# A two-layer diffusion backbone on one core: where layer 0's second shift is computed, FFN tile 1, fills, and the last squares

## The chip, the cores and the metric

The kernel runs on one core of one Trainium2 chip. The metric is the device time of one execution in microseconds (us). Three timed runs of the kernel before took 3376.17, 3380.72 and 3391.68 us; the median is 3380.72.

The engines are named as in the profile: PE is TensorE (matmul), DVE is VectorE, ACT is ScalarE, POOL is GpSimd, and SP is SyncE, which here only issues DMAs, from one queue in order.

## What is computed

The kernel computes two layers on a stream of 1024 latent tokens and 256 context tokens with 1024 columns, and returns the latents after a last RMSNorm. Cut to what matters here, a layer of the reference is:

```python
mod = c_act @ w_ada[li] + b_ada[li]
sh1, sc1, g1, sh2, sc2, g2 = jnp.split(mod[:, None, :], 6, axis=-1)
# (the same with cc_act for the context tokens)
m = unpack(modulate(rms_norm(x, norm1_w[li]), sh1, sc1) @ w_in[li], lb_all[li])
att  = diff_head_norm(diff_attend_blocks(rope(q), k_all, v_all, lam), ...)   # 4 heads
rec  = hgrn_out(hgrn_bidir(...), ...)             # gated linear recurrence, 4 heads
four = fourier_mix(m['uf'], w_fnet[li])           # FNet: 2-D Fourier mixing
x = x + g1 * (concat(att, rec, four) @ w_out[li])
x = x + g2 * conv_ffn(modulate(rms_norm(x, norm2_w[li]), sh2, sc2),
                      w_up[li], conv_w[li], conv_b[li], w_down[li])
# after the last layer: rms_norm(x, final_norm_w)
```

`w_ada` is 1024 x 6144 in each layer. The six parts of `mod` are shift, scale and gate of the first norm, then shift, scale and gate of the second. In tiles of 128 outputs, 24 to 31 are the second shift, 32 to 39 the second scale, 40 to 47 the second gate.

## The kernel before

**Products.** All large products run as three products of parts: a weight is split into a rounded part `wh` and the rest `wl`, an activation into `hh` and `hl` (`mt`: both in one tile), and PE adds wh x hh, wh x hl and wl x hh. Weights come as 128 x 1024 tiles (`wr`); ACT makes `wh`, and POOL or DVE subtracts to get `wl`.

**Stages of a layer.** The norm; the input projection as `head(h)` (q and k of one attention head, tile `g`, L378), `gemm_v(j)` (values, tile `gv`, L395) and others, spilled to memory; between them the hgrn pairs 0 and 1 (`hgrn_pair`), whose small chains on DVE and ACT are covered by filling PE with projections (`fill0`, `fill1`); FNet (`vp` L822, `sp`, `pq`, `fps`); the rope work of each head, `late(h)`, which loads spilled q and k, rotates them on POOL and writes them to memory places `zk`, `zq`, `zl`; attention (scores `sp` L913, maximum on DVE, exponential on ACT, transposes `tp`, outputs `op` L961); the output projection (`wout_all`), with the second norm's squares beside it; the FFN's up phase (`phase_up`), 22 pairs of column tiles; the down phase (`phase_down`) in pairs of tiles.

**Memory.** Tiles come from pools that are opened and closed like a stack on two sides. The hgrn pool closes when the last instruction on its tiles is done. FNet's pool, the rope pool and the attention tiles take the place that it leaves.

**The adaLN product** is no matmul for most tiles: a row of the transposed weight block is multiplied on DVE with the broadcast condition and summed up in the same instruction. It is spread over the program as generators that are advanced from the code of other stages. `ada_halves` (layer 0, tiles 16 to 31, from the hgrn stage): a step is one load `adaq` of two tiles' quarter, 256 KB, and four products of 128 x 256 (L246: two tiles, two conditions); 32 steps, two load buffers, which it shares with hgrn's `kts`. `ada_wout` (layer 0, tiles 32 to 39, from the output projection): a load `adaw` of 512 KB and two products of 128 x 1024 a tile (L149). `ada_rest` (tiles 40 to 47 of layer 0 and 0 to 31 of layer 1, from layer 0's FFN): 160 steps of one load of 128 KB and one or two products of 128 x 256 (L223), advanced by `fill` behind certain DVE instructions of the up phase and by one behind each of the eight columns of a down pair.

**The up phase** uses a scheme with seven products in place of eight for a 2 x 2 block of weights: `begin` and `more` make the products pE and pA of a tile, `regular` makes pD, `second` the products on sums of weights (`q`) with sums of activations (`xt`, `t`, made by `Blocks` after the norm), pB and pE. `split` makes the two parts of a weight; every third of its results goes to an own tile `wl2`, which for layer 0 lies in the FFN pool. `context` (tile `gc`) is the plain product for the context tokens. `Rstd` gathers a norm's squares: ACT squares a column tile, DVE or POOL adds it to `acc` (L291) or it is left as a further part, and `finish` sums over the partitions with a matmul by ones (`ss`, L300) and makes the reciprocal root on ACT (L301, L302).

**Order.** The kernel is written with a tile framework whose scheduler simulates a timeline and from it sets the order of every engine's instructions; an engine then runs its list in order, and waits on semaphores where a tile isn't ready.

Of the kernel before, what the change touches and what calls it, by code (L numbers as in the profile page):

```python
# [75 lines left out]
def backbone(ctx: ExitStack, tc: tile.TileContext, xt, cvec, wada, wada0, win, winv, wout, wup, wdown, wfn,  # L76
# [200 lines left out]
    class Rstd:  # L277


        def __init__(self, acc, tmp):  # L280
            self.acc, self.tmp, self.seen, self.more = acc, tmp, set(), {}

        def add(self, x, t0, n, eng=None):
            r = slice(t0, t0 + n)
            if t0 in self.seen:
                sq = self.tmp(n)
                S.activation(out=sq[:, :n], in_=x[:, r], func=AF.Square)
                if eng is PE:
                    self.more.setdefault(t0, []).append(sq)
                    return  # L290
# [4 lines left out]

        def finish(self, ps, t0, n):
            r = self.acc[:, t0:t0 + n]
            parts = [r] + self.more.get(t0, [])
            for i, a in enumerate(parts):
                PE.matmul(ps[:, :n], lhsT=ones, rhs=a[:, :n], start=(i == 0), stop=(i == len(parts) - 1))  # L300
# [66 lines left out]
    def mixers(l, hs, hpool, epool, ep, hside, oside):  # L367
# [4 lines left out]
        with tc.tile_pool(name=f"psx{l}", bufs=3, space=PSUM) as psx, tc.tile_pool(name=f"psg{l}", bufs=3, space=PSUM) as psg:  # L372
# [32 lines left out]
            if True:  # L405
                with tc.tile_pool(name=f"hgrn{l}", bufs=1, side=oside) as gp:
                    mark("hgrn0")
                    ada = ada_halves(gp, 0, (0, 1), range(16, 32)) if l == 0 else none(gp)

                    def pace(*counts):  # L410
                        todo = iter(counts)

                        def also():
                            for _ in range(next(todo, 0)):
                                next(ada, None)
                        return also
                    hgrn_pair(l, 0, gp, psx, gemm, gemm_v, both, qch, pace(2, 2, 2, 1, 1))
                    mark("fill0")
                    also = pace(*[1] * 8)
# [4 lines left out]
                    hgrn_pair(l, 1, gp, psx, gemm, gemm_v, both, qch, list)  # L424
                    mark("fill1")
                    also = pace(*[2] * 5 + [1] * 6)
# [173 lines left out]
    def hgrn_pair(l, p, gp, psx, gemm, gemm_v, both, qch, also):  # L600
# [42 lines left out]
        if p == 0:  # L643
            gemm_v(2, also)
# [450 lines left out]
    def phase_up(l, blocks, psp, pcp, nrm, q, p1):  # L1095
# [19 lines left out]
        def split(x, r=slice(0, 1024)):  # L1115
            turn_w[0] += 1
            h = wp.tile([P, 1024], F32R, tag="wh", name="wh")
            w = (nrm if last else fp).tile([P, 1024], F32R, tag="wl2", bufs=1, name="wl") if turn_w[0] % 3 == 0 else wp.tile([P, 1024], F32R, tag="wl", bufs=2, name="wl")
# [37 lines left out]
        def more(j):  # L1156
            j.A = bank("pA")
            product(j.A, j.w1, 512, blocks.B21, True)
            j.c1 = context(j.w1)
            j.w1 = None  # L1160
# [58 lines left out]
        def gate(j):  # L1219
            j.g, done = conv(j.f, u1, j.c1)  # L1220
            fill(done, 1)
# [19 lines left out]
        more(j)  # L1241
        yield
        regular(j)
        ahead = None
        if last:
            ahead = begin(1)
            more(ahead)
# [8 lines left out]
        for f in range(1, NF):  # L1256
# [4 lines left out]
            if not ahead:  # L1261
                more(j)
            ahead = None
# [16 lines left out]
    def phase_down(l, xs, hs, psp, pcp, cvs, norm_of, acts, rest):  # L1280
# [11 lines left out]
        def down(fs):  # L1292
            ws = [(load_w(wdown[l, f]), a) for f, a in fs]
            for d in range(KD):
# [8 lines left out]
                fill(done, 1)  # L1303
# [413 lines left out]
```

## Time and profile before

| what | value |
|---|---|
| timed runs | 3376.17, 3380.72, 3391.68 us |
| profiled execution | 3365.03 us, its span 3363.2 us |
| mean granted TensorE clock | 0.962 |
| PE busy | 3073.5 us (91%) |
| DVE busy | 2407.3 us (72%) |
| ACT, POOL busy | 1389.9 us (41%), 1087.7 us (32%) |
| DMA | 397.75 MB, mean 118 GB/s |

How to read the views below. A *window* row gives its bounds and length in us, then the busy time (and the number of instructions) of PE, PEld (weight loads beside PE), DVE, ACT and POOL, the mean granted TensorE clock as a share of full speed (2.4 GHz), the DMA engines' busy share, and GB/s. The *clock slices* of the page cut the span into 40 parts of 84 us and give the clock in tenths. A *source* row gives line, engine, operation and tiles of a group, how often it ran, the shortest, median and longest duration in ns, the first and last start in us, and the shapes; under it stand the releasers of the idle time just before these instructions, in us and how often. A *wait* row says who waited for whom: us in total, how often, the longest. A *timeline* row gives start, duration, engine, line, operation and tiles, and in brackets the engine's idle time before it with what ended it. Large matmuls appear as two records for each instruction at full width.

The stages of layer 0 on the time axis of this execution: hgrn pair 0 with its fills to about 290, pair 1 to 470, FNet and the rest of the projections to 597, attention to 843, the output projection to 980, the FFN's up phase to about 1575, the down phase behind it.

### The profile page before, as it was taken

Reading aid. Unit: us, or ns where it says so; the run is one execution under the profiler, and the core shown is the slowest. Engines: PE = TensorE matmul, PEld = TensorE weight load, DVE = VectorE, ACT = ScalarE, POOL = GpSimd, SP = SyncE. Lnnn points to the kernel's source line nnn. Section 1 sums busy time; section 2 is a strip of 40 time slices with the busy share of each in tenths; the row PEclk is TensorE's granted clock in tenths of the full one; section 3 lists DMA queues with packets and bytes.
Section 4 is the critical chain, followed back from the end, with each engine's and each line's share of the span. In section 5 each row is a group of like instructions: output and inputs, shape, how many; then the busy total and the mean of one; then the engine's idle time right before and its main releaser. Section 6 shows DMA issues by size and latency. Waiting matters only on the chain.

```text
span 3363.2 us, 49615 instructions
## 1 busy us (share of the span) xinstructions
PE 3073.5 (91%) x19008; PEld 2562.8 (76%) x19008; DVE 2407.3 (72%) x3917; ACT 1389.9 (41%) x2360; POOL 1087.7 (32%) x742
## 2 busy tenths in 40 slices
PE   5899896799979999999899998998899899999998
PEld 3777775588867887877788786777787778887786
DVE  7467755698578888778877847763896877777546
ACT  5343421477244443334111453622673454444213
POOL 5253443561121111113432234444641111112643
PEclk8899997899989999999999998999999999999999
DMA  5223136665512222225432222136656222224421
GB/s 211 90 73 97 49 106 190 196 167 173 202 58 90 88 93 83 93 88 185 144 126 82 85 79 68 59 105 217 174 168 247 85 82 79 84 76 150 145 76 69
DMA packets 197505, 397.75 MB, mean 118 GB/s; under 512 B 21394, under 2 KB 94866, under 8 KB 197268
## 3 DMA queue, kind: packets, MB, share of 16 engines
q1 hardware_dynamic: 197268, 394.59, 36.1%
q8 instruction: 149, 2.44, 0.3%
q14 instruction: 88, 0.72, 0.1%
HBM read 284.66 MB, written 85.20 MB: 110 GB/s over the span
## 4 chain that ended last, share of the span: by engine, by line
PE 39%; DVE 17%; DMA 5%; issue 4%; ACT 2%; POOL 2%; SPq 0%; DVEq 0%; POOLq 0%; ACTq 0%
PE gl L1300 12%; PE pE L1129 7%; PE pB L1129 4%; DVE wl L1120 4%; PE g L378 3%; DMA wr<-wup 3%; PE gl L547 2%; PE gv L395 2%; DVE adaj L223 2%; PE pA L1129 2%; PE gc L1300 1%; DVE cv L1215 1%; PE op L961 1%; PE sp L913 1%; PE gl L1319 1%
## 5 line engine op out<-in xcount | busy, mean ns | idle before, releaser
L131 POOL TENSOR_TENSOR wl<-wr,wh 128x1024 fp32r<-128x1024 f32 x116 | 297.3, 2572 | 814.3 <-PE gc L1300 153.2
L1300 PE MATMUL gl<-mt,wh 128*128 128x512 f32 x1280 | 347.9, 396 | 15.2 <-DVE xs L1301 13.3
L1301 DVE SCALAR_TENSOR_TENSOR xs<-gl,mod,xs 128x512 f32<-128x512 f32 x336 | 235.8, 744 | 138.6 <-PE gl L1300 137.1
L129 ACT CAST wh<-wr 128x1024 fp32r<-128x1024 f32 x116 | 121.4, 1047 | 481.5 <-PE gc L1300 161.7
L1300 PEld LDWEIGHTS gl<-mt,wh 128*128 128x128 f32 x1280 | 235.7, 189 | 66.9 <-DVE xs L1301 16.8
L378 PE MATMUL g<-hh,wh 128*128 128x512 f32 (+1 forms) x696 | 257.3, 379 | 12.3 <-DVE w L597 9.2
L378 PE MATMUL g<-hl,wh 128*128 128x512 f32 (+1 forms) x696 | 255.8, 377 | 0.0
L1129 PE MATMUL pE<-mt,wh 128*128 128x512 f32 x704 | 229.8, 397 | 1.5 <-ACT u L1179 1.5
L915 DVE TENSOR_REDUCE mx<-sp 128x1 f32<-128x1280 f32 (+1 forms) x136 | 194.3, 1436 | 47.9 <-PE sp L913 47.2
L1120 DVE TENSOR_TENSOR wl<-wr,wh 128x1024 fp32r<-128x1024 f32 (+1 forms) x134 | 214.2, 1606 | 13.1 <-ACT wh L1119 7.5
L923 ACT ACTIVATE e<-sp,mx 128x1280 f32<-128x1280 f32 (+1 forms) x144 | 177.9, 1238 | 64.5 <-DVE mx L915 63.4
L1300 PE MATMUL gl<-mt,wl 128*128 128x512 f32 x640 | 190.8, 395 | 0.0
L1119 ACT CAST wh<-q 128x1024 fp32r<-128x1024 f32 x44 | 46.2, 1051 | 311.7 <-DVE q L1165 247.1
L961 PE MATMUL op<-vt,at 128*128 128x128 f32 x1312 | 161.3, 278 | 4.9 <-ACT at L951 4.2
L223 DVE SCALAR_TENSOR_TENSOR adaj<-adaq,cq 128x256 bf16<-128x256 f32 x256 | 160.3, 626 | 6.2 <-DMA adaq<-wada 5.3
L378 PEld LDWEIGHTS g<-hh,wh 128*128 128x128 f32 x696 | 135.7, 195 | 37.6 <-issue 6.4
L1119 ACT CAST wh<-wr 128x1024 fp32r<-128x1024 f32 (+1 forms) x134 | 129.4, 971 | 81.1 <-PE pB L1129 46.7
L1129 PE MATMUL pE<-mt,wl 128*128 128x512 f32 x528 | 148.9, 399 | 14.7 <-DVE wl L1120 14.7
L961 PEld LDWEIGHTS op<-vt,at 128*128 128x128 f32 x1312 | 153.6, 193 | 10.4 <-ACT at L951 9.8
L378 PE MATMUL g<-hh,wl 128*128 128x512 f32 (+1 forms) x696 | 158.7, 366 | 0.0
L1129 PEld LDWEIGHTS pE<-mt,wh 128*128 128x128 f32 x704 | 133.2, 189 | 32.5 <-ACT u L1179 2.4
L378 PEld LDWEIGHTS g<-hl,wh 128*128 128x128 f32 x696 | 135.6, 195 | 23.4 <-issue 0.2
(312 smaller groups left out, 7804.6 us busy)
## 6 DMA issues: line engine op xcount, KB each, us to landing
wr<-wup SPq DMA_DIRECT2D x88, 512.0 KB, 3.7
wr<-wdown SPq DMA_DIRECT2D x44, 512.0 KB, 3.7
adaq<-wada SPq DMA_DIRECT2D x160, 128.0 KB, 2.2
wr<-win SPq DMA_DIRECT2D x36, 512.0 KB, 3.7
rp<-rope SPq DMA_DIRECT2D x32, 512.0 KB, 4.9
wr<-wout SPq DMA_DIRECT2D x24, 512.0 KB, 4.6
mgd<-mp SPq DMA_DIRECT2D x24, 512.0 KB, 4.0
adaw<-wada SPq DMA_DIRECT2D x24, 512.0 KB, 6.1
```

The costliest lines, as they stand in the source:

```text
L129: S.copy(out=hi[:, :n], in_=raw[:, :n])
L131: G.tensor_tensor(out=lo[:, :n], in0=raw[:, :n], in1=hi[:, :n], op=ALU.subtract)
L223: V.scalar_tensor_tensor(out=junk, in0=raw, scalar=1.0, in1=cqs[si], op0=ALU.mult, op1=ALU.mult, accum_out=part[:, si, q, i:i + 1])
L378: PE.matmul(ps[:, :n], lhsT=a, rhs=b[:, t0:t0 + n], start=(i == 0), stop=(i == 3 * KD - 1))
L915: V.reduce_max(out=w["mx"][:, c, :m], in_=sp.rearrange("p (k t) -> p k t", t=nk), axis=AX.X, negate=True)
L923: S.activation(out=e[:, k * nk:(k + 1) * nk], in_=w["sp", c][:, k * nk:(k + 1) * nk], func=AF.Exp, bias=w["mx"][:, c, k:k + 1], accum_out= ...
L961: heads["mm"] = PE.matmul(op[:, k, :], lhsT=w["at"][:, k * nb + j, :], rhs=hd["vt"][:, j, :], start=(j == 0), stop=(j == nb - 1))
L1119: S.copy(out=h[:, r], in_=x[:, r])
L1120: V.tensor_tensor(out=w[:, r], in0=x[:, r], in1=h[:, r], op=ALU.subtract)
L1129: PE.matmul(ps, lhsT=a[:, c + k * P:c + (k + 1) * P], rhs=b, start=(first and i == 0), stop=(i == len(todo) - 1), skip_group_check=True)
L1300: PE.matmul(ps[:, :n], lhsT=a, rhs=b[:, r], start=(j == 0), stop=(j == len(terms) - 1))
L1301: done = V.scalar_tensor_tensor(out=xs[d][:, r], in0=ps[:, :n], scalar=modcol(l, 0 if t0 else 1, 5, d), in1=xs[d][:, r], op0=ALU.mult, op1 ...
```

## The change

Six places are changed.

1. `ada_halves` computes tiles 16 to 23 instead of 16 to 31: 16 steps instead of 32. The list of paces is gone. `hgrn_pair` gets no steps; `fill0` and `fill1` take one step for each chunk of a projection, so that 12 stand in `fill0` and 4 in `fill1` (before: 8 in pair 0's `gemm_v(2)`, 8 in `fill0`, 16 in `fill1`).
2. `ada_wout` computes tiles 24 to 39 in layer 0, in five batches (before 32 to 39 in four): 16 loads and 32 products instead of 8 and 16.
3. In the up phase, tile 1's `begin` and `more` are called ahead in both layers (before in the last alone), and its context product follows later (`first_context`). The tile `wl2` is taken by splits 4, 7, 10, ... instead of 3, 6, 9, ....
4. Behind `gate`, an even tile advances `ada_rest` by two steps instead of one.
5. In the down phase, the first two pairs advance `ada_rest` by nothing.
6. In the last layer's last 256 tokens, all squares but the first go to PE as parts of the sum (before four were added on DVE); `some` issues the products of parts already there between the down products, into one bank kept from column 0 on.

```diff
-                    ada = ada_halves(gp, 0, (0, 1), range(16, 32)) if l == 0 else none(gp)
...
-                    hgrn_pair(l, 0, gp, psx, gemm, gemm_v, both, qch, pace(2, 2, 2, 1, 1))
+                    ada = ada_halves(gp, 0, (0, 1), range(16, 24)) if l == 0 else none(gp)
+
+                    def also():
+                        next(ada, None)
+                    hgrn_pair(l, 0, gp, psx, gemm, gemm_v, both, qch)
                     mark("fill0")
-                    also = pace(*[1] * 8)
                     head(1, also)
...
                     mark("fill1")
-                    also = pace(*[2] * 5 + [1] * 6)
                     gemm_v(0, also)
...
-            w = (nrm if last else fp).tile([P, 1024], F32R, tag="wl2", bufs=1, name="wl") if turn_w[0] % 3 == 0 else wp.tile([P, 1024], F32R, tag="wl", bufs=2, name="wl")
+            w = (nrm if last else fp).tile([P, 1024], F32R, tag="wl2", bufs=1, name="wl") if turn_w[0] % 3 == 1 and turn_w[0] > 1 else wp.tile([P, 1024], F32R, tag="wl", bufs=2, name="wl")
...
         def gate(j):
             j.g, done = conv(j.f, u1, j.c1)
-            fill(done, 1)
+            fill(done, 2 - j.f % 2)
...
         regular(j)
-        ahead = None
-        if last:
-            ahead = begin(1)
-            more(ahead)
+        ahead = begin(1)
+        more(ahead)
...
-                fill(done, 1)
+                if others:
+                    fill(done, 1)
...
-                        norm.add(xs[d], t0, n, G if ci < 2 and d % 2 == 0 else PE if t0 == 1024 and d > 3 else V)
+                        if t0 == 1024 and last:
+
+                            if d == 0:
+                                norm.ps = psp.tile([P, 512], F32, tag="s", name="ss")
+                            if d > 1:
+                                norm.some(norm.ps, t0, n)
+                            norm.add(xs[d], t0, n, PE)
+                        else:
+                            norm.add(xs[d], t0, n, G if ci < 2 and d % 2 == 0 else V)
...
-        for size in [1] + [2] * 9 + [1] if last else [2] * 10:
-            down(todo[:size])
+        for i, size in enumerate([1] + [2] * 9 + [1] if last else [2] * 10):
+            down(todo[:size], i > 1)
...
-        n0 = 32
-        for n1 in (34, 36, 38, 40) if l == 0 else (36, 40, 43, 46, 48):
+        n0 = 24 if l == 0 else 32
+        for n1 in (28, 31, 34, 37, 40) if l == 0 else (36, 40, 43, 46, 48):
...
-            norm.finish(psp.tile([P, 512], F32, tag="s", name="ss"), *late)
+            norm.finish(norm.ps, *late)
```

**Where the instructions stand now.** DVE at the end of `fill1` and the start of FNet, layer 0, before (L246 are the adaLN products, `mod` their sums, `zl` a tile of the rope stage, `ue`, `uo` and `fa` FNet's inputs):

```order
L246 SCALAR_TENSOR_TENSOR adaj,part<-adaq,cq 128x256 x6
L782 TENSOR_TENSOR o<-o,sq 128x256
L246 SCALAR_TENSOR_TENSOR adaj,part<-adaq,cq 128x256 x18
L254 TENSOR_TENSOR mod_0_87<-mod_0_87,part 128x16
L254 TENSOR_TENSOR mod_1_88<-mod_1_88,part 128x16
L246 SCALAR_TENSOR_TENSOR adaj,part<-adaq,cq 128x256 x32
L254 TENSOR_TENSOR mod_0_87<-mod_0_87,part 128x16
L254 TENSOR_TENSOR mod_1_88<-mod_1_88,part 128x16
L264 TENSOR_TENSOR mod_0_87<-mod_0_87,sm 128x16
L264 TENSOR_TENSOR mod_1_88<-mod_1_88,sm 128x16
```

The same place after:

```order
L246 SCALAR_TENSOR_TENSOR adaj,part<-adaq,cq 128x256 x6
L781 TENSOR_TENSOR o<-o,sq 128x256
L246 SCALAR_TENSOR_TENSOR adaj,part<-adaq,cq 128x256 x2
L254 TENSOR_TENSOR mod_0_87<-mod_0_87,part 128x8
L254 TENSOR_TENSOR mod_1_88<-mod_1_88,part 128x8
L264 TENSOR_TENSOR mod_0_87<-mod_0_87,sm 128x8
L264 TENSOR_TENSOR mod_1_88<-mod_1_88,sm 128x8
L438 MEMSET zl 64x1280
L439 MEMSET zl 64x1280
```

Of the 64 products behind the last hgrn rows, 16 are left (8 stand some rows above either piece), so that `zl` and FNet's first rows follow 48 products earlier.

PE at FNet's first product in layer 0 (`vp`), before, behind the last product of `gemm_v(1)`:

```order
L395 MATMUL gv<-wh,hl 128x256
L395 MATMUL gv<-wl,hh 128x256 x8
L822 MATMUL vp<-cm,fa 128x128 x8
L833 MATMUL sp_5270<-u_5264,cm 128x2
L834 MATMUL sp_5270<-u_5264,cm 128x1
L840 MATMUL pq<-dm,ve 128x256 x8
```

After, `vp` stands among the products `g` of head 3, ahead of all of `gemm_v(1)`:

```order
L384 MATMUL g<-hl,wh 128x512
L384 MATMUL g<-hh,wh 128x512
L821 MATMUL vp<-cm,fa 128x128 x8
L832 MATMUL sp_5110<-u_5104,cm 128x2
L833 MATMUL sp_5110<-u_5104,cm 128x1
L384 MATMUL g<-hl,wh 128x512
```

FNet's products moved from behind the projections of head 3 and `gemm_v(1)` (`g` and `gv`) into them.

PE at the start of the FFN of layer 0, before (pD is tile 0's, pE and pA at 128 x 512 x8 and x4 are tile 1's, pB and `gc` tile 0's):

```order
L1129 MATMUL pD<-mt,wh 128x512 x8
L1129 MATMUL pD<-mt,wl 128x512 x4
L1129 MATMUL pD<-mt,wh 128x512 x8
L1129 MATMUL pD<-mt,wl 128x512 x4
L1129 MATMUL gc<-mt,wh 128x256 x8
L1129 MATMUL pB<-xt,wh 128x512
L1129 MATMUL pE<-mt,wh 128x512 x8
L1129 MATMUL pA<-mt,wh 128x512 x8
L1129 MATMUL pE<-mt,wl 128x512 x4
L1129 MATMUL pA<-mt,wl 128x512 x4
L1129 MATMUL gc<-mt,wl 128x256 x4
L1129 MATMUL gc<-mt,wh 128x256 x2
```

After:

```order
L1128 MATMUL pD<-mt,wh 128x512 x8
L1128 MATMUL pD<-mt,wl 128x512 x4
L1128 MATMUL pD<-mt,wh 128x512 x8
L1128 MATMUL pD<-mt,wl 128x512 x4
L1128 MATMUL pE<-mt,wh 128x512 x8
L1128 MATMUL pE<-mt,wl 128x512 x4
L1128 MATMUL pA<-mt,wh 128x512 x8
L1128 MATMUL pA<-mt,wl 128x512 x4
L1128 MATMUL gc<-mt,wh 128x256
L1128 MATMUL pB<-xt,wh 128x512
```

Tile 1's 24 products moved ahead of the context product `gc` and of the first pB.

## Rows read from the trace of the kernel before

**Rows 1.** The page: busy time of the engines, and the clock slices.

```profile
PE 3073.5 (91%) x19008; PEld 2562.8 (76%) x19008; DVE 2407.3 (72%) x3917; ACT 1389.9 (41%) x2360; POOL 1087.7 (32%) x742
...
PEclk8899997899989999999999998999999999999999
```

**Rows 2.** Windows: hgrn's end to attention, attention; layer 0, layer 1.

```profile
469.80:633.60 163.80, 111.46 (x594) 92.53 (x594) 76.68 (x231) 28.27 (x52) 59.26 (x45) 0.80 0.62 187
...
633.60:842.70 209.10, 196.44 (x1406) 172.58 (x1405) 181.79 (x247) 152.83 (x352) 88.26 (x63) 1.00 0.56 168
...
2251.20:2357.20 106.00, 96.29 (x554) 81.00 (x553) 38.16 (x67) 28.56 (x44) 44.36 (x32) 0.97 0.70 220
...
2357.20:2553.00 195.80, 183.00 (x1305) 162.78 (x1304) 168.65 (x205) 137.97 (x290) 91.01 (x63) 0.98 0.58 170
```

**Rows 3.** FNet product of line 822, its idle time, and a wait of the scores.

```profile
L822 PE MATMUL vp<-cm,fa x48: 272/399/582, 545.7 to 589.3; 128*128 128x128 f32 x32, 128*64 128x128 f32 x16
...
  DMA rp<-rope: 17.6, 1
...
PE sp L913 <- DMA zq<-hi: 12.2, 2, 10.9
```

**Rows 4.** Line 246 on DVE, 440 to 560, and its idle time.

```profile
L246 DVE SCALAR_TENSOR_TENSOR adaj<-adaq,cq x64: 412/421/1031, 461.0 to 533.9; 128x256 f32<-128x256 f32 x64
...
  DMA adaq<-wada: 46.7, 15
```

**Rows 5.** Last hgrn norm products in either layer, attention's output products, rope on GpSimd.

```profile
L775 PE MATMUL ss<-sq,cs x4: 377/380/483, 452.7 to 469.8; 128*128 128x256 f32 x4
...
L775 PE MATMUL ss<-sq,cs x8: 377/377/484, 2210.0 to 2251.2; 128*128 128x256 f32 x8
...
L961 PE MATMUL op<-vt,at x672: 270/275/377, 633.6 to 842.7; 128*128 128x128 f32 x168
...
L472 POOL TENSOR_SCALAR hi<-raw x12: 853/1490/1927, 544.8 to 657.0; 128x512 fp32r<-128x512 f32 x8, 128x256 fp32r<-128x256 f32 x4
...
  DMA raw<-pj: 43.3, 2
```

**Rows 6.** Waits of PE and of DVE, 60 to 170.

```profile
PE g L378 <- DVE w L597: 6.0, 1, 6.0
...
DVE adaj L246 <- DMA adaq<-wada: 18.1, 6, 5.1
```

**Rows 7.** Line 246 on DVE, 280 to 345, and its idle time.

```profile
L246 DVE SCALAR_TENSOR_TENSOR adaj<-adaq,cq x32: 399/421/2597, 294.2 to 333.7; 128x256 f32<-128x256 f32 x32
...
  DMA adaq<-wada: 11.4, 7
```

**Rows 8.** Windows of the output projection, layer 0, and line 149 there.

```profile
858.30:897.00 38.70, 38.70 (x205) 32.90 (x204) 35.42 (x60) 8.84 (x13) 9.36 (x3) 1.00 0.78 289
...
897.00:942.10 45.10, 45.10 (x250) 38.73 (x249) 17.53 (x23) 12.95 (x20) 14.39 (x6) 1.00 0.33 108
...
L149 DVE SCALAR_TENSOR_TENSOR junk<-adaw,cb x16: 1207/1217/3021, 864.0 to 895.1; 128x1024 f32<-128x1024 f32 x16
```

**Rows 9.** Timeline at the end of the first FFN hole: DVE, PE.

```profile
1012.43 1.23 DVE L1120 TENSOR_TENSOR wl<-q,wh 128x1024 fp32r<-128x1024 f32 x1 [5.71 <-POOL t L1075]
...
1013.71 2.08 PE L1129 MATMUL pB<-xt,wl 128*128 128x512 f32 x4 [11.20 <-DVE wl L1120]
```

**Rows 10.** A wait of DVE in the up phase, 1080 to 1560.

```profile
DVE q L1164 <- DMA wr<-wup: 89.9, 18, 7.0
```

**Rows 11.** First down pairs, 1575 to 1660: a wait of PE, line 223.

```profile
PE gl L1300 <- DVE xs L1301: 13.3, 3, 8.7
...
L223 DVE SCALAR_TENSOR_TENSOR adaj<-adaq,cq x32: 406/426/3145, 1573.3 to 1658.7; 128x256 bf16<-128x256 f32 x32
```

**Rows 12.** Timeline of the end: PE, ACT.

```profile
3349.07 1.22 PE L300 MATMUL ss<-acc,cs 128*128 128x256 f32 x2 [5.47 <-DVE acc L291]
...
3353.57 0.47 ACT L301 ACTIVATE acc<-ss,eps_t 128x256 f32<-128x256 f32 x1 [4.63 <-PE ss L300]
```

More of the change, by code (lines that the diff above doesn't have):

```diff
@@ L280, in __init__ @@
         def __init__(self, acc, tmp):
-            self.acc, self.tmp, self.seen, self.more = acc, tmp, set(), {}
+            self.acc, self.tmp, self.seen, self.more, self.done = acc, tmp, set(), {}, {}
         def add(self, x, t0, n, eng=None):
@@ L288, in add @@
                 if eng is PE:
-                    self.more.setdefault(t0, []).append(sq)
+                    self.more.setdefault(t0, []).append(sq[:, :n])
                     return
@@ L294, in add, with some @@
                 S.activation(out=self.acc[:, r], in_=x[:, r], func=AF.Square)
+        def some(self, ps, t0, n, end=False):
+            i = self.done.get(t0, 0)
+            parts = [self.acc[:, t0:t0 + n]] + self.more.get(t0, [])
+            for j in range(i, len(parts) - (not end)):
+                PE.matmul(ps[:, :n], lhsT=ones, rhs=parts[j], start=(j == 0), stop=(end and j == len(parts) - 1), skip_group_check=True)
+            self.done[t0] = max(i, len(parts) - (not end))
         def finish(self, ps, t0, n):
             r = self.acc[:, t0:t0 + n]
-            parts = [r] + self.more.get(t0, [])
-            for i, a in enumerate(parts):
-                PE.matmul(ps[:, :n], lhsT=ones, rhs=a[:, :n], start=(i == 0), stop=(i == len(parts) - 1))
+            self.some(ps, t0, n, True)
             S.activation(out=r, in_=ps[:, :n], func=AF.Ln, scale=1.0 / D, bias=eps_t)
@@ L407, in mixers @@
                     mark("hgrn0")
-                    ada = ada_halves(gp, 0, (0, 1), range(16, 32)) if l == 0 else none(gp)
[L410 to L416, printed above, removed]
-                    hgrn_pair(l, 0, gp, psx, gemm, gemm_v, both, qch, pace(2, 2, 2, 1, 1))
+                    ada = ada_halves(gp, 0, (0, 1), range(16, 24)) if l == 0 else none(gp)
+                    def also():
+                        next(ada, None)
+                    hgrn_pair(l, 0, gp, psx, gemm, gemm_v, both, qch)
                     mark("fill0")
-                    also = pace(*[1] * 8)
                     head(1, also)
@@ L423, in mixers @@
                     mark("hgrn1")
-                    hgrn_pair(l, 1, gp, psx, gemm, gemm_v, both, qch, list)
+                    hgrn_pair(l, 1, gp, psx, gemm, gemm_v, both, qch)
                     mark("fill1")
-                    also = pace(*[2] * 5 + [1] * 6)
                     gemm_v(0, also)
@@ L598, in logsig, with hgrn_pair @@
         return g, w
-    def hgrn_pair(l, p, gp, psx, gemm, gemm_v, both, qch, also):
+    def hgrn_pair(l, p, gp, psx, gemm, gemm_v, both, qch):
         last = l == DEPTH - 1
@@ L643, in hgrn_pair @@
         if p == 0:
-            gemm_v(2, also)
+            gemm_v(2)
         for g in (0, 2, 6):
@@ L1158, in more, with first_context @@
             product(j.A, j.w1, 512, blocks.B21, True)
+        def first_context(j):
             j.c1 = context(j.w1)
@@ L1241, in phase_up @@
         more(j)
+        first_context(j)
         yield
         regular(j)
[L1244 to L1247 removed]
+        ahead = begin(1)
+        more(ahead)
         fp, cvs, rest, u2 = yield
@@ L1262, in phase_up @@
                 more(j)
+            first_context(j)
             ahead = None
@@ L1290, in fill, with down @@
                     pass
-        def down(fs):
+        def down(fs, others):
             ws = [(load_w(wdown[l, f]), a) for f, a in fs]
```

## Prediction

> **What bounds the kernel now.** I read the page first: TensorE is busy 91% of the span and VectorE 72% [rows 1]. So only the places where PE stands still, or runs at its lower clock, can give time back; work that lies beside a busy PE costs nothing. The row of the PE clock is lowest, at 7 tenths, in its seventh slice of 84 us, from about 505 [rows 1]. I then cut the time before attention into a table of windows, the same stretch in both layers, from the last hgrn norm product to attention's first output product. Layer 0 takes 163.80 us for 111.46 us of PE work at a mean clock of 0.80; layer 1 takes 106.00 us for 96.29 at 0.97 [rows 2]. PE's rows name the hole: the FNet product `vp` began at 545.7 after standing 17.6 us, and the first latent scores stood 12.2 us [rows 3]. The code says what came before. The hgrn pool cannot close before the adaLN stream (L246) is done, and the FNet, rope and attention tiles lie in the memory it gives back. Through 461.0 to 533.9 that stream is 64 products of 0.42 us, and DVE stood 46.7 us for their loads, 15 times [rows 4]: it is bound by load latency with two buffers, one step of two tiles each 4.6 us (72.9 us over 16 steps). PE's last hgrn product was at 469.8 [rows 5]. So for 64 us after PE was ready to go on, a chain of small loads held the memory.
>
> **The change part by part**, in order of time, against the profiled execution.
>
> *hgrn pair 0.* Eight steps leave (the eight of `gemm_v(2)`). PE waited 6.0 us behind DVE's `w` there, and DVE itself 18.1 us for the loads [rows 6], in front of that `w` in its row order. Smaller waits beside it may go too. I take -7, range -10 to -3.
>
> *hgrn pair 1.* Twelve steps stand in the fill before it instead of eight, with the last of them among DVE's `kt`, `LA` and `LB` rows. What is queued behind each is that chain, and PE's `sp` products wait for it. Eight steps held DVE 11.4 us in 7 waits and 13.5 us in their own products (32 x 0.421, from 294.2 to 333.7) [rows 7]; four more are half of each, 12.5 us, and most meets gaps of DVE. Ends 0 and +12; I take +4, nearer to nothing since the loads are asked for earlier than their rows.
>
> *Fill 1, FNet, start of attention.* Of 16 steps from 461 on, four remain: the chain ends after about 4 x 4.6 us, at 479, not 534. Then nothing of layer 0 differs in kind from layer 1, and PE's new order shows it: FNet's products now stand among the products of head 3 and of `gemm_v(1)`, where before they were behind all of them. So I price the stretch by layer 1: at best its 106.00 us (-58), with layer 0's own busy time, which its larger FNet and its low clock make longer, 111.46 + the 9.71 that PE idles in layer 1 = 121.2 (-43); the middle is -50, and I take -48. Attention itself idles the same in both layers (209.10 - 196.44 = 12.66, 195.80 - 183.00 = 12.80 [rows 2]) and is left as it is. Bounds: -58, and -35 if the 12.2 us wait for `zq` stays.
>
> *Output projection.* Eight more tiles: 16 more products with accumulation (L149), and 8 more loads of 512 KB on SP's queue, ahead of later `wout` loads. The 16 now there lie between 864.0 and 895.1, at 1.217 us, the worst 3.021 [rows 8]. PE is busy without a gap in both windows; DVE has 38.70 - 35.42 = 3.3 us free in the first and 45.10 - 17.53 = 27.6 in the second [rows 8]. Sixteen at 1.3 us with the accumulator's read are 21 us, at the worst price 48. So the cover holds at the usual price; without it the term is 48 - 30.9 = +17. I take 0, nearest to the median row. What waits for them is the norm's scale, needed only at the end of that window.
>
> The worst product, 3.021 beside a median of 1.217, stands in the window in which GpSimd is busy for 9.36 us [rows 8]. The Trainium skill ("SBUF — State Buffer", section "Who interferes with whom") says that a VectorE instruction with two SBUF inputs and a GpSimd instruction that reads SBUF exclude each other for the whole instruction, and the one that comes second stands. By this rule the added products could lose at most GpSimd's busy time in the two windows, 9.36 + 14.39 = 23.8 us; with their own 21 that is 45 against 30.9 of room, and the term would be up to +14 instead of 0. The worst of the sixteen lost 1.8 us and the middle one nothing, with GpSimd as busy then as after: no run here yet shows the whole of it, and I don't take it.
>
> *Second FFN tile ahead.* PE's 24 matmuls of tile 1 (`pE`, `pA`) moved from behind the first `pB` and half of `gc` to right behind `pD`. Both places lie inside the same hole: PE waits 11.20 us for `wl`, whose subtraction waits 5.71 us until GpSimd's `t` is done and the pool under it free [rows 9]. The splits are renumbered, but the tile of `q` gets `wl2` again (the fourth split instead of the third), so the same chain ends the hole and the same PE work lies within. I take 0, range -5 to +4.
>
> *Gate fill.* Eleven more steps in layer 0's up phase, two products of 0.42 us each: 9.5 us of DVE. They come just ahead of DVE's 18 waits for `wup`, 89.9 us together, 5 each [rows 10], so 0.86 hides in 5. Where it does not, the whole 9.5 counts. I take +3, range 0 to +10; SP's queue gets 11 loads of 128 KB.
>
> *First two down pairs.* PE waited 13.3 us for DVE's `xs`, with 32 adaLN products in the window, one of them 3.145 us [rows 11]. Without them DVE has room. The later pairs still hold all steps: 99 + 64 places for 160. I take -8, range -13 to -2.
>
> *Last norm.* PE's five `ss` products began at 3349.07 after 5.47 us of waiting for DVE's additions, and ACT's logarithm came at 3353.57 [rows 12]. After, the squares go straight to PE, and DVE has no additions for them: three of eight products stand among the `gl`, five at the end as before, of which only the last must wait for the last column's sum and square. So the 4.5 us of products stay and nearly all of the 5.47 go: -5, range -7 (some products hidden too) to 0 (PE waits for each square instead).
>
> Sum: -7 + 4 - 48 + 0 + 0 + 3 - 8 - 5 = **-61 us**. The profiled execution took 3365.03 with a span of 3363.2; it lies 15.7 under the median of 3380.72. 3365.0 - 61 = 3304, and with the 15.7 back the median is about **3319 us**.
>
> **The rivals.** (1) *Rope holds attention.* FNet goes early, but the first scores wait for head 0's rope, pieces of loads and GpSimd work behind each other with two buffers. For it: the 12.2 us wait of `sp` for `zq`, and GpSimd's 43.3 us for `raw` [rows 3, 5]. Against: layer 1 has the same pieces and 9.71 us of idle in all. Price: only the 17.6 goes, the sum is -61 + 48 - 18 = -31, 3350 us. (2) *Slower: SP's one queue.* The rope pieces' loads now stand among the weight loads of head 3 and `gemm_v(1)`. If a load that waits for its buffer holds the weights behind it, PE's 58 us of those products (469.8 to 545.7 - 17.6) come after the rope work instead of ahead of it. Rope began 11 after the chain's end (544.8 - 533.9), so at 490 now; to attention's first output it was 88.8 more (633.6 - 544.8); with the 58 behind it and the 43.3 of waiting for `raw` a second time that is 680, against 633.6: +47, with the other terms' -13 a sum of +34, 3415 us. It decides for slower from the point where attention's first output comes later than 647. Against: layer 1's queue is mixed the same way at 0.97 clock. (3) *The small terms are covered or go against:* hgrn pair 1 +12, output projection +17, gate fill +10, down -2, end 0: -7 + 12 - 48 + 17 + 10 - 2 + 0 = -18, 3363 us.
>
> **How the numbers follow.** Forecast 0.74, rope 0.12, small terms 0.08, SP's queue 0.03, nothing at all 0.03. The likeliest one's own range is -80 to -40 (its bounds added in part), 3301 to 3341. The whole range reaches up to the first rival and down to nearly all best ends together (-10 + 0 - 58 - 5 + 0 + 0 - 13 - 7 = -93): 3292 to 3352. About 0.5% (17 us) is what a measurement here can tell from no change. Faster by more: forecast, rope and half of the small terms, 0.90; same 0.06; slower 0.04.
>
> **What would show it.** In the new profile: DVE's last L246 product near 479; `vp` products among head 3's `g`, without the 17.6 us wait; a clock near 0.97 from hgrn's end to attention's first output, which comes some 113 us after the last norm product; L149 32 times up to about 925 with PE still whole; the hole of about 16 us at the start of the FFN unchanged; no wait of 8.7 us on `xs` in the first down pairs; the last `ss` within 4 us of the last `gl`. Attention's first output later than 620 on the old time axis would make the prediction wrong, and so would a new PE gap of over 10 us under the output projection.

## The result, and the profile after

The changed kernel takes **3321.48 us** (median of 4 runs, 3320.46 to 3327.40); the kernel before, run beside it, took 3378.44 (4 runs, 3367.72 to 3391.68). The ratio is 0.9837, with a 95% interval of 0.9814 to 0.9860: 1.6% faster. 3319 was forecast.

The two profiled executions lie only 38 us apart, 3325.6 against 3363.2 us of span, since that of before (3365.03) was quicker than all its timed runs, and that of after (3327.40) the slowest of its four. So the places below add up to 38 and not to 57. The table gives the time of the same event in four traces: before, and the shift against it in the changed kernel, in a second trace of the changed kernel, and in the quickest version of the experiments (the second tile not ahead, in its second trace).

| event (PE) | before | after | after, again | not ahead |
|---|---|---|---|---|
| first `ops` product of hgrn pair 0 | 226.2 | -16.3 | -13.9 | -15.5 |
| end of the last hgrn norm product, pair 1 | 470.2 | -4.1 | -2.5 | -3.4 |
| attention's last output, layer 0 | 842.9 | -44.5 | -42.0 | -43.8 |
| end of pD, start of the FFN | 982.2 | -44.7 | -41.4 | -43.8 |
| last pE, end of the up phase | 1571.5 | -34.5 | -25.9 | -36.6 |
| first product of layer 1 | 1905.0 | -39.6 | -32.6 | -51.8 |
| attention's last output, layer 1 | 2553.3 | -37.0 | -25.8 | -51.7 |
| last down product | 3343.6 | -32.3 | -22.7 | -49.2 |
| last norm product | 3353.5 | -39.7 | -30.2 | -56.6 |

So hgrn pair 0 gained 16 us and pair 1 lost 12; FNet and attention gained 40; the output projection nothing; the up phase lost 10; the down phase gained 5; layer 1, up to its last down product, lost 7; the last norm product gained 7, of which 2 are lost again behind it. The page after, clock slices (to [rows 1]; PE is busy 92%, DVE 71%):

```profile
PEclk8989999999989999999999998999999999999999
```

The low tenth of the seventh slice is gone. Windows of the trace after. The third and fourth answer to layer 0's two in [rows 2], the fifth and sixth to the windows of [rows 8]:

```profile
100.00:130.00 30.00, 30.00 (x180) 26.78 (x180) 19.01 (x30) 18.10 (x34) 7.17 (x5) 1.00 0.17 60
221.70:275.00 53.30, 49.34 (x606) 37.74 (x606) 40.75 (x69) 18.72 (x41) 28.44 (x33) 0.87 0.22 71
465.80:575.00 109.20, 98.73 (x593) 83.55 (x592) 50.97 (x133) 28.34 (x53) 47.38 (x35) 0.98 0.71 221
575.00:798.50 223.50, 200.50 (x1406) 175.55 (x1405) 189.45 (x247) 153.20 (x352) 99.26 (x72) 0.98 0.57 170
814.00:852.00 38.00, 38.00 (x200) 32.24 (x199) 34.83 (x54) 8.84 (x13) 9.11 (x3) 1.00 0.86 316
852.00:898.00 46.00, 46.00 (x255) 39.53 (x254) 38.38 (x64) 13.14 (x20) 16.91 (x6) 1.00 0.53 178
937.50:1536.90 599.40, 560.32 (x2828) 468.07 (x2827) 478.84 (x843) 244.86 (x303) 73.72 (x27) 0.97 0.27 90
```

From the last hgrn norm product to attention's first output it is 109.20 us instead of 163.80, at a clock of 0.98 instead of 0.80; attention behind that is 14 us longer. Some windows of the trace before that were not shown: pair 0 around its wait, the last part of pair 0, and the up phase:

```profile
100.00:140.00 40.00, 30.56 (x159) 25.95 (x157) 26.57 (x87) 16.91 (x32) 7.17 (x5) 0.88 0.35 110
238.00:285.00 47.00, 43.88 (x606) 33.86 (x606) 40.71 (x69) 18.63 (x41) 28.53 (x33) 1.00 0.24 79
982.20:1571.50 589.30, 554.24 (x2833) 464.95 (x2834) 473.43 (x793) 244.09 (x303) 75.28 (x28) 0.98 0.27 89
```

Line 246 on DVE in the trace after, 440 to 560, with its idle time (to [rows 4]), FNet's first product (to [rows 3]) and attention's outputs (to [rows 5]):

```profile
L246 DVE SCALAR_TENSOR_TENSOR adaj<-adaq,cq x16: 415/422/609, 456.9 to 471.6; 128x256 f32<-128x256 f32 x16
...
  DMA adaq<-wada: 7.1, 3
```

```profile
L821 PE MATMUL vp<-cm,fa x48: 270/275/323, 488.4 to 539.0; 128*128 128x128 f32 x32, 128*64 128x128 f32 x16
```

```profile
L960 PE MATMUL op<-vt,at x672: 270/275/421, 575.0 to 798.2; 128*128 128x128 f32 x168
```

The adaLN chain ends at 472 instead of 534, and `vp` starts at 488.4 with no idle time in front of it. That the chain held memory, and not only its place in DVE's list, shows in FNet's first load (`wf`, a tile of the place that the hgrn pool leaves), which SP issued right behind the chain's last sum before, and 59 us earlier after:

```profile
534.62 0.34 SPq L788 DMA_DIRECT2D wf<-wfn  x1
```

```profile
475.58 0.33 SPq L787 DMA_DIRECT2D wf<-wfn  x1
```

Before pair 1, the steps in the trace after (to [rows 7]; 47 of 48 records):

```profile
L246 DVE SCALAR_TENSOR_TENSOR adaj<-adaq,cq x47: 394/421/2614, 284.2 to 347.6; 128x256 f32<-128x256 f32 x47
...
  DMA adaq<-wada: 16.3, 10
```

The scores' waits in layer 0's attention (to [rows 3]):

```profile
PE sp L912 <- DMA zq<-hi: 4.4, 1, 4.4
...
PE sp L912 <- DMA zl<-lw: 2.7, 1, 2.7
```

Line 149 in the output projection (to [rows 8]): all 32 products run up to 883.7, in windows in which PE is busy from end to end.

```profile
L149 DVE SCALAR_TENSOR_TENSOR junk<-adaw,cb x32: 1207/1217/3303, 819.9 to 883.7; 128x1024 f32<-128x1024 f32 x32
```

Six of the 32 took 2.7 to 3.3 us. Each of these began while GpSimd subtracted for a weight (`wl`, L131) and ended 1.08 us behind that subtraction. One of the six on DVE, and GpSimd's subtraction, which ended at 844.04:

```profile
842.10 3.02 DVE L149 SCALAR_TENSOR_TENSOR junk<-adaw,cb 128x1024 f32<-128x1024 f32 x1
```

```profile
841.18 2.87 POOL L131 TENSOR_TENSOR wl<-wr,wh 128x1024 fp32r<-128x1024 f32 x1 [10.80 <-PE gc L546]
```

The hole at the FFN's start, DVE and PE (to [rows 9]), is as long as it was, 11.40 against 11.20 us:

```profile
966.77 1.23 DVE L1119 TENSOR_TENSOR wl<-q,wh 128x1024 fp32r<-128x1024 f32 x1 [5.70 <-POOL t L1074]
```

```profile
968.05 1.22 PE L1128 MATMUL pB<-xt,wl 128*128 128x512 f32 x2 [11.40 <-DVE wl L1119]
```

New is a wait in the first down pair: PE's product there waits 5.65 us for the rounding of the second activation (`mt`, L1090).

```profile
1544.69 1.22 PE L1301 MATMUL gl<-mt,wh 128*128 128x512 f32 x2 [5.65 <-ACT mt L1090]
```

What came before it on GpSimd, on SP (`acc` is the second activation's load; the line under it is that load's time to landing), and on ACT:

```profile
1526.80 2.40 POOL L131 TENSOR_TENSOR wl<-wr,wh 128x1024 fp32r<-128x1024 f32 x1 [3.40 <-ACT mt L1090]
1529.15 2.95 POOL L1091 TENSOR_TENSOR mt<-acc,mt 128x1280 fp32r<-128x1280 f32 x1
```

```profile
1530.27 1.75 SPq L1340 DMA_DIRECT2D xs<-xmd  x4
1532.13 0.67 SPq L1083 DMA_DIRECT2D acc<-actd  x1
...
DMA to landing us min/median/max: 10.3/10.3/10.3
```

```profile
1542.09 1.28 ACT L1230 ACT_TABLE_LOAD   x1
1543.38 1.26 ACT L1090 CAST mt<-acc 128x1280 fp32r<-128x1280 f32 x1
```

GpSimd subtracts for a weight before it makes the first activation's rest (L1091), which ends at 1532.1. The second activation's load goes out right behind that, after four loads of `xs` on the same queue, and lands 10.3 us later, at 1542.4. On ACT the rounding stands behind a table load and starts 0.9 us after the landing, so ACT's own order costs under 1 us; the rest of the wait is the late load.

The end, PE (to [rows 12]): the last norm product ends 2.5 us behind the last down product (3311.3), where it was 9.9. From there to the end of the span it is 11.8 us instead of 9.7.

```profile
3311.58 1.03 PE L301 MATMUL ss<-p,cs 128*128 128x256 f32 x4
3312.45 1.37 PE L301 MATMUL ss<-q,cs 128*128 128x256 f32 x4
```

### The profile page after: what moved, and what is told of

It reads as the page before. It is cut to its first block, busy times and chain, and to the rows that moved or that the text cites. A ratio compares the mean times of both kernels' runs of the same rounds, so it can differ in the third digit from the quotient of the medians.

```text
span 3325.6 us, 49540 instructions
## 1 busy us (share of the span) xinstructions
PE 3075.6 (92%) x19014; PEld 2563.6 (77%) x19014; DVE 2364.7 (71%) x3820; ACT 1391.6 (42%) x2360; POOL 1092.0 (33%) x742
## 4 chain that ended last, share of the span: by engine, by line
PE 41%; DVE 16%; DMA 6%; issue 3%; ACT 3%; POOL 2%; SPq 0%; DVEq 0%; POOLq 0%; ACTq 0%
PE gl L1301 13%; PE pE L1128 7%; PE g L384 5%; DVE wl L1119 4%; PE pB L1128 3%; DMA wr<-wup 3%; PE gl L546 2%; PE gv L401 2%; PE gc L1301 2%; DVE adaj L223 2%; PE pA L1128 2%; DVE cv L1216 1%; PE sp L912 1%; PE op L960 1%; DVE cv L1217 1%
## 5 line engine op out<-in xcount | busy, mean ns | idle before, releaser
L131 POOL TENSOR_TENSOR wl<-wr,wh 128x1024 fp32r<-128x1024 f32 x116 | 300.1, 2597 | 790.3 <-PE gc L1301 168.5
L1119 DVE TENSOR_TENSOR wl<-wr,wh 128x1024 fp32r<-128x1024 f32 (+1 forms) x134 | 196.4, 1474 | 3.2 <-ACT wh L1118 1.8
L1128 PE MATMUL pE<-xt,wh 128*128 128x512 f32 x352 | 143.0, 406 | 9.6 <-DVE xt L1074 9.6
```

The source lines that it names most:

```text
L131: G.tensor_tensor(out=lo[:, :n], in0=raw[:, :n], in1=hi[:, :n], op=ALU.subtract)
L1119: V.tensor_tensor(out=w[:, r], in0=x[:, r], in1=h[:, r], op=ALU.subtract)
L1128: PE.matmul(ps, lhsT=a[:, c + k * P:c + (k + 1) * P], rhs=b, start=(first and i == 0), stop=(i == len(todo) - 1), skip_group_check=True)
```

## The experiments

The kernels were run in three groups, each beside the kernel before on one chip. The changed kernel's ratio was 0.9837 in the result and 0.9845 in the third group (below); differences between groups below 0.002 are not read.

**The second shift back in the hgrn stage** (the first two edits undone):

```diff
-                    ada = ada_halves(gp, 0, (0, 1), range(16, 24)) if l == 0 else none(gp)
+                    ada = ada_halves(gp, 0, (0, 1), range(16, 32)) if l == 0 else none(gp)
...
-                    hgrn_pair(l, 0, gp, psx, gemm, gemm_v, both, qch)
+                    hgrn_pair(l, 0, gp, psx, gemm, gemm_v, both, qch, pace(2, 2, 2, 1, 1))
...
-        n0 = 24 if l == 0 else 32
-        for n1 in (28, 31, 34, 37, 40) if l == 0 else (36, 40, 43, 46, 48):
+        n0 = 32
+        for n1 in (34, 36, 38, 40) if l == 0 else (36, 40, 43, 46, 48):
```

> The changed kernel with the second shift's eight tiles back in the hgrn stage (steps in pair 0, both fills) and the output projection as before; all other edits stay. Theory (the gain comes from the adaLN chain that held the hgrn pool): FNet's first product waits again some 17 us, attention ends about 42 us later than in the changed kernel, and the whole is 40 to 50 us slower than it, near 3367. Rival (the gain is mostly in the FFN and the end): within 10 us of the changed kernel, near 3325.

Measured: 3376.05 against 3376.56 us, ratio 0.9991 (0.9979 to 1.0003). Without this part nothing is left of the gain. FNet's first product begins at 548.2, PE waits 23.6 us for FNet's inputs in five waits (18.0 the longest), and attention ends 2.6 us later than before, 47 later than in the changed kernel. The other four edits together come to 3 us, which the interval doesn't tell from nothing. This run undoes the steps of both pairs and of the second fill at once; what each of them is worth is read from the traces alone.

**One step behind each gate:**

```diff
-            fill(done, 2 - j.f % 2)
+            fill(done, 1)
...
-            down(todo[:size], i > 1)
+            down(todo[:size], i > 0)
```

> The changed kernel with one adaLN step behind each gate, and fills left out in the first down pair only (so that all 160 steps still have a place). Theory (the 11 extra steps of the gates lengthen PE's waits for wl and u and with them drop its clock, which cost some 11 us in the up phase): 6 to 11 us faster there, 4 given back in the second down pair; near 3316. Rival (the renumbered wl2 and the tile ahead cost it): the up phase stays as long, the whole is 3 to 5 us slower, near 3325.

Measured: 3310.92, ratio 0.9805 (0.9793 to 0.9818). The window of the up phase, from pD's end to the last pE, in this kernel:

```profile
934.00:1522.80 588.80, 553.67 (x2827) 463.55 (x2826) 470.93 (x796) 244.03 (x303) 73.61 (x27) 0.98 0.27 90
```

588.80 us, as long as before (589.30) and 10.6 shorter than after. The wait for the second activation is still there in the first down pair, in a kernel that is among the quickest:

```profile
PE gl L1301 <- ACT mt L1090: 6.2, 2, 6.0
```

**The second tile not ahead:**

```diff
-        ahead = begin(1)
-        more(ahead)
+        ahead = None
+        if last:
+            ahead = begin(1)
+            more(ahead)
...
-            w = (nrm if last else fp).tile([P, 1024], F32R, tag="wl2", bufs=1, name="wl") if turn_w[0] % 3 == 1 and turn_w[0] > 1 else wp.tile([P, 1024], F32R, tag="wl", bufs=2, name="wl")
+            w = (nrm if last else fp).tile([P, 1024], F32R, tag="wl2", bufs=1, name="wl") if turn_w[0] % 3 == 0 else wp.tile([P, 1024], F32R, tag="wl", bufs=2, name="wl")
```

> The changed kernel with the second tile not ahead in layer 0 and wl2 taken by splits 3, 6, 9 as before; the rest stays. Theory (the hole at the FFN's start is the same either way, the extra 11 us of the up phase are the gates'): within 3 us of the changed kernel, 3321. Rival (the renumbering costs): the up phase 8 to 11 us shorter, near 3312.

Measured: 3307.86, ratio 0.9802 (0.9789 to 0.9814). The theory fell, the rival's time came true, though not its place: the up phase (595.5) is four us shorter, which is within what traces of the same code differ by, and eight are in the down phase, where PE no longer waits for the rounding.

**Steps in the first two down pairs again** (`down(todo[:size], True)`):

> The changed kernel with adaLN steps in the first two down pairs again. Theory (those steps made PE wait for xs): PE waits 8 to 13 us more there, the whole 8 us slower, near 3329. Rival (PE's waits there come from GpSimd and DVE work at the change of phase): within 2 us, 3321.

Measured: 3330.23, ratio 0.9855 (0.9841 to 0.9870). PE's waits in the first pairs of this kernel:

```profile
PE gl L1301 <- ACT mt L1090: 5.7, 1, 5.7
PE gl L1301 <- DVE xs L1302: 2.1, 1, 2.1
PE gc L1301 <- DVE xs L1302: 1.9, 2, 1.5
```

The time from the last pE to layer 1's first product is 333.9 us, against 328.5 after and 333.5 before: the steps are worth 5 us, and PE's waits for `xs` 4.0, where 8 to 13 were expected. The largest wait, for the rounding, is there with and without them.

**The tile not ahead, but the new rotation of `wl2`** (the first half alone of the edit under "The second tile not ahead"):

> The changed kernel with the second tile not ahead in layer 0, but wl2 taken by splits 4, 7, 10 as in the changed kernel. Theory A (the tile ahead alone displaced the order at the end of the up phase): as fast as the version with both undone, near 3308, and PE has no wait of 5 to 6 us for the second activation's rounding on ACT in the first down pair. Theory B (the rotation of wl2 did it): near 3321, with that wait.

Measured: 3326.48, ratio 0.9834 (0.9811 to 0.9857). PE's wait in the first down pairs of this kernel:

```profile
PE gl L1303 <- ACT mt L1090: 5.9, 2, 5.7
```

Theory B: beside the gates' two steps, the new rotation costs the time, with or without the tile ahead. The tile ahead with the old rotation was not tried (its third split would lie in a pool that is not open yet).

**Gates and rotation undone together** (the edits under "One step behind each gate" and "The second tile not ahead"):

> The changed kernel with both the gates' extra steps (and the fill of the second down pair) and the tile ahead with its rotation undone. Theory (two separate costs, 11 and 12 us): 3298 to 3302, up phase of layer 0 within 2 us of the kernel before. Rival (one and the same waiting, which either undoing removes): 3306 to 3310.

Measured: 3323.02, ratio 0.9815 (0.9791 to 0.9839): no faster than either alone, within the intervals. The up phase is 593.2 us; the second down pair has its steps again, and PE waits 8.3 us for `xs` in the first ones (2.8 without). The costs don't add: with one step behind each gate, the rotation costs nothing that the intervals show (0.9805 with it, 0.9815 without).

**Eight and eight steps in the two fills** (on top of the last one):

```diff
+                    left = [8]
+
                     def also():
-                        next(ada, None)
+                        if left[0]:
+                            left[0] -= 1
+                            next(ada, None)
...
                     mark("fill1")
+                    left[0] = 99
```

> As the version with gates and tile ahead undone, and of the 16 adaLN steps of the hgrn stage 8 stand in the first fill and 8 in the second (12 and 4 in the changed kernel). Theory (four steps among pair 1's rows cost 6 us; four more in the second fill keep the pool 18 us longer, but PE has 58 us of projections to do by then): 3 to 6 us faster than that version. Rival (FNet and rope start 18 us later and attention with them): 8 to 12 us slower than it.

Measured: 3318.67, ratio 0.9806 (0.9782 to 0.9830). Pair 1's end comes 7.8 us earlier than in the last kernel, at 460.0, with 32 products among its rows instead of 47; the first scores come at 561.0 as there (560.8), since the second fill is longer; FNet's first product comes at 500.3 instead of 490.1. Attention ends 3.8 earlier. About half of the gain is given back at the pool, where the rival had more than all of it given back. In the time (0.9806 against 0.9815) the two kernels are not told apart.

**Rope of head 1 ahead of the output projection's weights** (on the changed kernel):

```diff
-            ws = [load(d) for d in ds]
+            with tc.issue_after(rope_done[l, 1].ins):
+                ws = [load(d) for d in ds]
```

(`rope_done[l, 1]` is GpSimd's last subtraction of head 1's rope; the edit holds for GpSimd's queue alone.)

> The changed kernel, with GpSimd's two subtractions for the first output-projection weights put behind head 1's rope work instead of ahead of it (in the changed kernel GpSimd stood 14.6 us in front of the first of them, for values' products on PE, while head 1's rope waited behind). Theory (this wait delays head 1's rope, and the scores' 4.4 and 2.7 us waits for zq and zl follow from it): both waits vanish, attention in layer 0 ends 5 to 7 us earlier, 3315. Rival (the rope pieces are held by their loads, 30.4 us of GpSimd's waiting): same waits, 3321.

Measured: 3328.92, ratio 0.9838 (0.9814 to 0.9861). The wait for `zq` is gone and that for `zl` stays. That the edit did it is not shown: five other traces, of kernels without it (one step behind each gate, both of not ahead, gates and rotation undone, eight and eight), have no wait for `zq` either. PE's wait there in this kernel:

```profile
PE sp L915 <- DMA zl<-lw: 3.4, 1, 3.4
```

From the first score to attention's last output it is 236.5 us instead of 240.2: 3.7, too small to show in the time, and with one step behind each gate, without the rope edit, it is 236.4.

**The changed kernel again, and not ahead beside it**, on one chip:

> The changed kernel itself, on the same chip as the three others of this call, so that differences of 10 us can be read between them. Theory: ratio to the kernel before 0.981 to 0.985, as at first.

> The version without the tile ahead and with the old rotation, beside the changed kernel. Theory (the rotation of wl2 moves the second activation's rounding on ACT behind three convolutions; PE waits 5.7 us for it and its clock falls): 8 us faster than the changed kernel. Rival (the 12 us of the first comparison were mostly the two chips): within 3 us of it.

Measured: 3328.65, ratio 0.9845 (0.9828 to 0.9861), and 3311.67, ratio 0.9789 (0.9775 to 0.9804). The intervals are apart: without the rotation the kernel is 17 us faster than the changed one and 2.1% faster than before, the lowest ratio that was run (that of one step behind each gate, 0.9793 to 0.9818, overlaps it).

GpSimd, SP with the load's time to landing, ACT and PE at the start of the down phase without the rotation: GpSimd makes the first activation's rest at once, the second's load goes out 5.5 us earlier on the time axis, ahead of the loads of `xs`, and lands in 4.0 us instead of 10.3. The rounding follows it, and the 5.7 us are gone.

```profile
1523.62 2.95 POOL L1091 TENSOR_TENSOR mt<-acc,mt 128x1280 fp32r<-128x1280 f32 x1 [3.45 <-ACT mt L1090]
```

```profile
1526.59 0.33 SPq L1083 DMA_DIRECT2D acc<-actd  x1
...
DMA to landing us min/median/max: 4.0/4.0/4.0
```

```profile
1529.86 1.05 ACT L129 CAST wh<-wr 128x1024 fp32r<-128x1024 f32 x1 [0.77 <-PE pB L1128]
1530.82 1.26 ACT L1090 CAST mt<-acc 128x1280 fp32r<-128x1280 f32 x1
```

```profile
PE gl L1303 <- DVE xs L1304: 2.8, 1, 2.8
```

Its up phase, 596.40 us, is 8.4 shorter than that of the changed kernel beside it (604.8, the longest of six traces with that code; the shortest, with the first down pairs' steps, is 595.7):

```profile
938.40:1534.80 596.40, 560.10 (x2833) 469.15 (x2834) 481.06 (x837) 244.58 (x303) 77.03 (x28) 0.97 0.28 91
```

**The last squares on DVE again** (the last edit undone):

> The changed kernel with the last norm's squares added on DVE as before. Theory: the last product of the norm comes 9.9 us behind the last down product instead of 2.5, the down products end 2 us earlier, together 5 us slower than the changed kernel. Rival (the end is set by the output's DMAs anyway): no difference.

Measured: 3331.66, ratio 0.9849 (0.9835 to 0.9862), 3 us above the changed kernel beside it, inside the intervals. The trace shows the place: the last norm product ends 10.1 us behind the last down product instead of 2.5, and PE waits as before:

```profile
PE ss L301 <- DVE acc L291: 6.7, 2, 5.5
```

**All together:** gates with one step, the old rotation, eight and eight, rope first.

> Gates with one step, no tile ahead with the old rotation, eight and eight steps in the hgrn fills, rope of head 1 ahead of the output projection's weights: all that the runs so far spoke for. Theory (the costs are separate: 5 of the gates, 8 of the rotation, 3 to 5 of the steps, 4 of the rope): 18 to 22 us faster than the changed kernel. Rival (what one frees, the next wait takes): about as fast as the version without the tile ahead alone, 8 to 12 us.

Measured: 3329.12, ratio 0.9844 (0.9822 to 0.9867): no gain. Attention in layer 0 takes 246.7 us from its first score, ten more than with rope first alone and 11 more than with eight and eight (235.6), from which this kernel differs by the rope edit alone. ACT's wait, and PE's for ACT, in this kernel:

```profile
ACT wh L129 <- DMA wr<-wout: 8.7, 1, 8.7
```

```profile
PE tp L957 <- ACT at L958: 7.6, 4, 6.8
```

The rounding of an output-projection weight stood on ACT in the middle of attention and waited 8.7 us for its load, and PE behind it. That wait is 4.3 us with rope first alone and 0.2 with eight and eight: moved off GpSimd's queue, the wait came up in ACT's.

## Why the prediction was right, and where it was not

The time, the direction and the cause held. Putting the second shift back takes the ratio from 0.9837 to 0.9991, 52 us, where the terms of the first two edits (-7, +4, -48, 0) come to 51; the other four edits were forecast at 10 and come to 3, not told from nothing. That it is the chain in the second fill, and the memory that it held, is read from the traces: its end, FNet's first load, `vp` and the clock moved together. Term by term, by the traces:

- **hgrn pair 0, -7:** measured -16 (-13.9 and -15.5 in the two other traces). PE's idle time in the window shown went, 9.4 us, 7.2 of it behind `w` [rows 6]. Most of the rest is clock, which I left out: around its 6 us wait PE ran at a mean of 0.88 in that window, and at 1.00 now, and up to the same place (196 before, 181 after) its busy time fell by 5.6.
- **hgrn pair 1, +4:** measured +12. Half is the steps, which now reach up to 347.6 instead of 333.7 [rows 7], and with 32 again (eight and eight) pair 1 ends 7.8 earlier. The other half is not the change's: in the last part of pair 0 the same 606 products took 49.34 us at 0.87 instead of 43.88 at 1.00. In the same stretch (222 to 275) the other traces show 0.87 to 0.94 in ten cases and 1.00 in two, the quick ones with the same code there as the changed kernel; among the ten is the kernel with the second shift put back, which has the old code there (0.90).
- **Fill 1 to attention, -48:** measured -40. Chain, `vp` and clock came as forecast, and attention's first output 109 us behind the last norm product, where I had 113. What failed is the step that left attention itself as it is: PE idles 23.0 us in it (223.50 - 200.50) where I left 12.66. I put my mark at its first output, which came 36 us after the first score before (597.1 to 633.6) and comes 17 after it now (558.3 to 575.0); and the scores then wait 4.4 and 2.7 us for head 1's rope, which the bound -35 had as a wait that might stay.
- **Output projection, 0:** measured -0.2. DVE was busy 34.83 of 38 and 38.38 of 46 us, PE whole. Six of the 32 products stood until a subtraction of GpSimd was over and lost 11 us together, where I had read one such product before (there were two, 3.01 and 3.02 us). The trace so agrees in kind with the Trainium skill's rule on the shared port ("SBUF — State Buffer", section "Who interferes with whom"), but the +14 that it would have allowed did not come: DVE had the room for the 11 us.
- **Second tile ahead, 0:** the hole is the same, as forecast, but the step was wrong as a whole: I followed the renumbered splits to the first hole and no further. With the rotation the scheduler's order is another some 560 us later, at the end of the up phase: on GpSimd a weight's subtraction stands before the first activation's rest, on SP the second activation's load behind those of `xs`. That cost 8 us there (328.5 and 326.8 us from the last pE to layer 1's first product, 320.2 and 318.4 without the rotation). Undone, it gives 12 us in the one comparison and 17 in the other, the largest error of the sum; but beside one step behind each gate it gives nothing, so the cost is not the rotation's alone.
- **Gate fill, +3:** the up phase is 10.1 us longer after, and as long as before with one step (588.8). The 10.1 are 6.1 us of PE's busy time (560.32 against 554.24, at a clock of 0.97 against 0.98) and 4.0 of its idle time. With the old rotation the second step costs little: 595.5 and 596.4 with it, 593.2, 595.1 and 596.2 without. So the two edits cost together; how much each would alone is not settled, since six traces of the same code lie between 595.7 and 604.8.
- **First down pairs, -8:** the steps were worth 5.4 (333.9 to 328.5), and without the rotation's new wait the stretch takes 318.4 and 320.2: -13 to -15.
- **Last norm, -5:** measured -7.4 from the last down product to the last norm product, of which 2.1 are given back behind it (11.8 us to the end of the span instead of 9.7): -5.3. Before, eight scalings of the last tokens were left for DVE there, in 2.77 us; after, ten take 8.64, beside GpSimd's.

The errors of pair 0 (-9), pair 1 (+8), attention (+8), the up phase (+7) and the down phase (+3) come to +17 against the forecast, and layer 1, for which there was no term, came out 7 longer, so that the two traces lie 38 us apart and not 61. That the median fits within 3 us is therefore partly luck: errors of both signs met, and the trace of before lies 13.4 us under its median and that of after 5.9 over its own, which brings the 38 to the 57 of the medians.

## What to carry to other kernels

A chain of small loads with two buffers need not cost anything where PE has other work, but look at what its pool holds: here the last of 32 steps kept the place of three later stages (FNet, rope, attention). When a change renumbers buffers in a kernel whose order a scheduler makes, compare the order of every engine to the very end, and not only at the place that is meant. When an engine waits for a row, look at when that row's input landed before blaming its place in the list. Take waits off one at a time: of the four edits beside the two that counted, each with a reason, the sum was worth nothing; undoing either of two of them gave over 10 us, and undoing both gave no more than that.

## What was not expected of the hardware

The clock is a term of its own. A wait of 6 us behind `w` lay in a window at a mean of 0.88, between the two levels. In the up phase after, four windows of 16 us in which PE waited (3.8, 2.3, 1.9 and 2.0 us) show 0.89, but others with waits of 2.3 and 2.2 us stayed at 1.00, as did the trace before behind its first hole (1.9 at most). So the length of one wait does not tell whether the clock falls. Two such windows of the trace after:

```profile
1088.00:1104.00 16.00, 13.66 (x71) 11.27 (x70) 11.29 (x19) 3.70 (x5) 1.95 (x1) 1.00 0.26 88
1392.00:1408.00 16.00, 14.09 (x75) 12.07 (x74) 10.31 (x23) 5.96 (x8) 0.00 (x0) 0.89 0.27 103
```

The clock also moved in layer 1, whose code is the same in that place: from layer 1's first product to its attention's end it was 648.3 us before, 650.9 and 655.1 in the two traces of the changed kernel, and from 646.0 to 656.9 in the twelve traces with that code there. A difference of under 11 us between two single traces of such a stretch is thus no finding; where a shorter difference is read above, it stands in several traces or beside a wait that is in one and not in the other.
